# Last attention pair refilled with gates and modulation blocks, and attention results stored split

## The chip, the cores and the metric

The kernel runs on one core of one Trainium2 chip. The metric is device time in microseconds of one execution of the whole kernel: a median over repeated executions, and beside it one execution that was taken by the hardware profiler and from which every row of the trace comes. Engines are called as in the profile: PE (TensorE matmul), DVE (VectorE), ACT (ScalarE), POOL (GpSimd), SP (SyncE, which here issues most transfers).

## The reference

One layer of a hybrid network is computed for 64 sample tokens and 1024 prompt tokens (1088 columns in all), width 1024, in fp32. Cut to what the change touches:

```
mod  = silu(c) @ w_ada + b_ada                        # 48 blocks of 128 channels: shifts, scales, gates
u    = rmsnorm(x) * (1 + sc1) + sh1
proj = u @ w_in                                       # q, k, v, mLSTM inputs, and ga, gb (1024 each)
y_a  = stick_breaking(q, k, v)                        # 8 heads of 64, strictly causal
         z = q k^T / 8 ; a = sigmoid(z) * prod over later keys of sigmoid(-z) ; y = a v
y_b  = mlstm(...)                                     # 4 heads of 128
merged = sigmoid(ga) * (y_a @ w_a) + sigmoid(gb) * (y_b @ w_b)
x    = x + g1 * (merged @ w_out)
x    = x + g2 * ffn(rmsnorm(x) * (1 + sc2) + sh2)     # then a last rmsnorm
```

## The kernel before

Every matmul operand is split into a high part (rounded to the matmul format fp32r) and a low part (the rest), and one product is three matmuls: high by high, high by low, low by high (`mm3`). Activations lie transposed, channels on partitions, and the 1088 columns are walked in three token chunks of 320, 384 and 384.

The stages in order: modulation blocks 0 to 15, the norm and the operands `uh`, `ul`; the mLSTM branch, whose results go to `yb_d` in device memory already split; the attention stage, which is where the change lies; branch A (`y_a @ w_a`, merged with the rest); the output projection; the FFN; the last norm.

The attention stage works in four pairs of heads. `attention(p)` loads the operands of the two heads, then for a head takes eight query tiles of 128 in four steps m of two. For a query tile t: two matmuls for each 512 keys give `z` (PE), DVE adds the mask on the diagonal block, ACT takes two sigmoids, DVE runs a running product along the keys (the scan) and a multiply. Then PE transposes blocks of the result (`ps_a`), ACT rounds them (`ah`), DVE subtracts (`al`), PE multiplies with v (`po`), ACT and DVE put the two halves together in `ya`. Work grows with t: tile t has t+1 key blocks, 36 in a head and 72 in a pair. Between the two heads `sample()` does the 64 sample tokens against the cache. A pair ends with one store of `ya` to `ya_d`.

Beside it run *fillers*, work that needs nothing of attention: a gate unit (`gate_unit`: one 128-channel block of ga or gb over three chunks, 24 matmuls a chunk; ACT takes the sigmoid out of PSUM into a tile with the tag "gt", SP stores it) and modulation blocks (`ada_unit`: one 512 KB weight load, a few small matmuls). Gates and modulation blocks share two PSUM banks with the tag "d". There are 16 gates; two are done earlier, and the pairs 0, 1 and 2 get 5, 5 and 4 of them with 6, 8 and 8 modulation blocks. The last pair has the last eight modulation blocks and `branch_b` (24 products of 12 matmuls, which also use the "d" banks; each takes a gate tile back from memory, multiplies it on POOL and stores the product; two "gt" tiles each, of four). In three of its steps `branch_b` calls `load_y`, which brings back `ya` of the pairs 0 to 2 and splits it on POOL.

What sets the order: the program is written as generators. `run(consumer, dense, 27, 0)` with a last argument of 0 writes the whole consumer (the pair) first and then all its fillers. A scheduler then lays out a queue for each engine while the program is built: it takes what it holds to be ready by its own model, and what was written first goes first; tiles of one tag are given out in the order written. On the chip each engine runs its queue strictly in order. So the rows of a queue are a fact of the program, and only their times are open.

Of the kernel before, what the change touches and what calls it, by code (L numbers as in the profile page):

```python
# [35 lines left out]
def trunk(ctx, tc, a, o, dbg=None, stop=None):  # L36
# [105 lines left out]

    ya_d = dram.tile([3, P, T], F32, name="ya_d")
    yb_d = dram.tile([4, 2, P, T], F32, name="yb_d")
# [67 lines left out]

    def ada_blocks(blocks, tag, nb, load):

        n = len(blocks)
        i0, step = blocks[0], blocks[-1] - blocks[0]
        ps = bank(tag, f"ps_ada{i0}", nb)
        for b, i in enumerate(blocks):
            raw = load(i)
            nc.sync.dma_start(raw, cols(w_ada, i * P))  # L220
            for kb in range(KB):
                g = 32 * (kb % 4)
                nc.tensor.matmul(ps[g : g + 32, b * P : (b + 1) * P], cT[:, kb, :], raw[:, kb, :],
                                 start=kb < 4, stop=kb >= 4, tile_position=(0, g))
        sb = small([P, n * P], f"ada_sb{i0}", "adas")
        nc.vector.tensor_copy(sb, ps[:, 0 : n * P])
# [121 lines left out]

    def unit(name, fills, evac, alloc=None):
        wh, wl = w_unit(fills, name)  # L350
        if alloc:
            alloc()
        for c, (s, e) in enumerate(CHUNKS):
            ps = bank("d", f"ps_{name}_{c}", cur["d"])
            for kb in range(KB):
                mm3(ps[:, : e - s], wh[:, kb, :], wl[:, kb, :], uh[kb][:, s:e], ul[kb][:, s:e], kb == 0, kb == KB - 1)
            evac(ps, s, e)
            yield

    def w_cols(c0):  # L360
        return lambda raw: [(raw, cols(w_in, c0))]
# [82 lines left out]
    def attention(p):  # L444
# [73 lines left out]
        for i in range(2):  # L518
            qs, kh, kl, vs = hd[i]
            for m in range(4):  # L520
                avs = []
# [45 lines left out]
        if p < 3:  # L567
            nc.sync.dma_start(ya_d[p], ya)

# [255 lines left out]
    def gate_unit(b, c0, dst, name):  # L825
        def fin(ps, s, e):
            t = small([P, 384], f"gt_{name}{b}_{s}", "gt", bufs=cur["gt"])
            nc.scalar.activation(t[:, : e - s], ps[:, : e - s], AF.Sigmoid)  # L828
            nc.sync.dma_start(dst[b][:, s:e], t[:, : e - s])
        return unit(f"{name}{b}", w_cols(c0 + b * P), fin)  # L830

# [140 lines left out]
    def load_y(b):  # L972
        y_tiles(b)
        if b >= 4:
            for i, t in enumerate((yh[b], yl[b])):
                nc.sync.dma_start(t.bitcast(F32), yb_d[b - 4, i])
            return
        raw = up.tile([P, T], F32, tag="u", name=f"yr{b}")
        nc.sync.dma_start(raw, ya_d[b])
        for s, e in CHUNKS:  # L980
            hi_pool(yh[b][:, s:e], raw[:, s:e])
            lo_pool(yl[b][:, s:e], raw[:, s:e], yh[b][:, s:e])

# [6 lines left out]
    def branch_b():  # L990

        for m in range(KB):
            if m % 2 == 0:
                wh, wl = wb0 if m == 0 else wide_unit(w_b, 0, 4, m // 2, f"wb{m}")
            if 2 <= m < 5:
                load_y(m - 2)
            for c, (s, e) in enumerate(CHUNKS):
                n = e - s
# [11 lines left out]
    gi, ai = 2, 2  # L1010
    for p, (ng, na) in enumerate(((5, 6), (5, 8), (4, 8))):
        gs, ads = gates[gi : gi + ng], ada_left[ai : ai + na]
        gi, ai = gi + ng, ai + na
        fill = []
        for i in range(na):
            fill += gs[i : i + 1] + ads[i * na // ng : (i + 1) * na // ng]
        run(attention(p), chain(fill), 27, 0)
    wb0 = wide_unit(w_b, 0, 4, 0, "wb0")
    for b in range(4, 8):
        load_y(b)  # L1020
    run(attention(3), chain(ada_left[24:32] + [branch_b()]), 27, 0)
    ph.close()

# [34 lines left out]
    for m4 in range(0, KB, 4):  # L1058
        if m4:
            early_x = {m: wo_x(m) for m in range(2)}  # L1060
        was = [wide_unit(w_a, 0, 4, m // 2, f"wa{m}", hi_act, lo_dve) for m in (m4, m4 + 2)]
        for c, m in [(c, m4 + i) for c in range(3) for i in range(4)]:
# [682 lines left out]
```

## Time and profile before

| what | us |
|---|---|
| median of three executions (1789.58 to 1793.16) | 1790.57 |
| the profiled execution, its own time | 1792.89 |
| its span, first to last instruction | 1790.7 |
| mean granted TensorE clock | 0.984 |
| PE busy in the span | 1725.0 (96%) |
| DVE / ACT / POOL busy | 1039.5 / 745.5 / 539.0 |
| first matmul of attention pairs 0, 1, 2, 3 | 506.7, 591.2, 691.9, 784.4 |
| branch B, first to last matmul | 824.6 to 897.4 |
| branch A, first to last matmul | 897.6 to 949.1 |
| first matmul of the output projection | 949.2 |

Matmuls are pipelined and their ends are modelled, so PE counts as busy in the trace where it is merely in flight. The step from one matmul's start to the next is the better measure of what it costs, and that is what is used below. Times inside the trace are microseconds from the span's start.

### The profile page before, as it was taken

The page shows a single profiled execution, that of the slowest core. Times are in us where ns is not written, and L with a number is a line of the kernel's source. Part 1 is how long each engine was busy: PE and PEld are TensorE (multiplying, and loading weights), DVE is VectorE, ACT ScalarE, POOL GpSimd, SP SyncE. Part 2 cuts the span into 40 slices and gives each one's busy share as a digit, 9 for nine tenths or more (in the row PEclk, how much of TensorE's full clock was granted, in tenths as well). Part 3 has the DMA queues.
Part 4 walks back from the last instruction along what each step waited for, and adds up shares of the span by engine and source line. Part 5 has one row for each costly group of instructions (what it writes and reads, how often), then busy time and mean ns, then how long its engine had stood idle before and what let it go on. Part 6 is the DMA issues. An engine that isn't in the chain of part 4 may idle for free. (4 is left out here: it accounts for less than half of the span.)

```text
span 1790.7 us, 32772 instructions
## 1 busy us (share of the span) xinstructions
PE 1725.0 (96%) x12670; PEld 1661.6 (93%) x12670; DVE 1039.5 (58%) x2029; ACT 745.5 (42%) x1511; POOL 539.0 (30%) x491
## 2 busy tenths in 40 slices
PE   6999999999999999988899999999999999999998
PEld 4899999999989989877899999999999999999998
DVE  5533324152356858586554389666655677667964
ACT  6333333324234535353423457432333355453444
POOL 1434544445532232314656240044322100001000
PEclk9999999999999999998999999999999999999999
DMA  9436666664485565695576345744433588899942
GB/s 276 113 103 205 149 197 143 192 146 138 149 199 137 135 165 130 140 270 182 169 232 195 98 138 166 203 145 154 147 99 98 157 235 235 283 340 338 302 149 101
DMA packets 359534, 320.25 MB, mean 179 GB/s; under 512 B 16727, under 2 KB 327507, under 8 KB 359379
## 3 DMA queue, kind: packets, MB, share of 16 engines
q1 hardware_dynamic: 345074, 270.77, 50.2%
q0 software_dynamic: 14304, 47.39, 10.6%
q8 instruction: 100, 1.64, 0.4%
q14 instruction: 56, 0.45, 0.1%
HBM read 241.01 MB, written 98.09 MB: 189 GB/s over the span
## 5 line engine op out<-in xcount | busy, mean ns | idle before, releaser
L1627 PE MATMUL ps_d<-o,wh_d 128*128 128x272 f32 x1232 | 230.9, 287 | 0.8 <-DVE g L1388 0.8
L1627 PEld LDWEIGHTS ps_d<-o,wh_d 128*128 128x128 f32 x1232 | 192.7, 188 | 1.0 <-DVE g L1388 1.0
L1627 PE MATMUL ps_d<-o,wl_d 128*128 128x272 f32 x616 | 176.4, 288 | 0.0
L1627 PEld LDWEIGHTS ps_d<-o,wl_d 128*128 128x128 f32 x616 | 115.5, 188 | 0.0
L47 ACT CAST w<-wr 128x512 fp32r<-128x512 f32 x140 | 84.8, 618 | 66.3 <-PE ps_gc L1400 17.5
L56 DVE TENSOR_TENSOR w<-wr,w 128x512 fp32r<-128x512 f32 x140 | 95.5, 696 | 22.4 <-ACT w L47 20.1
L399 DVE TENSOR_TENSOR_SCAN re<-re 128x128 f32<-128x128 f32 (+3 forms) x64 | 100.8, 1577 | 13.1 <-ACT re L395 12.7
L1611 POOL DMA_DIRECT2D dsum_d<-wr_d x12 | 6.5, 538 | 240.5 <-DVE wr_d L1609 235.7
L395 ACT ACTIVATE re<-z 128x512 f32<-128x512 f32 (+2 forms) x96 | 47.4, 494 | 72.8 <-DVE z L391 59.2
L1400 PE MATMUL ps_ga<-b1h,w 128*128 128x272 f32 x352 | 74.7, 289 | 3.0 <-ACT g L1385 1.8
L1400 PE MATMUL ps_gc<-b5h,w 128*128 128x272 f32 x352 | 75.1, 292 | 1.1 <-DVE g L1388 1.1
L1400 PE MATMUL ps_gd<-b4h,w 128*128 128x272 f32 x352 | 74.1, 290 | 1.2 <-DVE hst L1382 1.2
L1400 PE MATMUL ps_gb<-b6h,w 128*128 128x272 f32 x352 | 74.2, 289 | 0.1
L1400 PE MATMUL ps_gd<-b7h,w 128*128 128x272 f32 x352 | 74.2, 290 | 0.0
L1400 PE MATMUL ps_gc<-b3h,w 128*128 128x272 f32 x352 | 73.7, 289 | 0.0
L1400 PE MATMUL ps_ga<-b2h,w 128*128 128x272 f32 x352 | 73.6, 288 | 0.0
L47 ACT CAST o<-hr 128x544 fp32r<-128x544 f32 x77 | 48.8, 645 | 52.0 <-DMA hr<-h_d 28.8
L47 ACT CAST wh_d<-wr_d 128x1024 fp32r<-128x1024 f32 (+1 forms) x42 | 41.1, 979 | 69.4 <-PE ps_d L1627 32.2
L76 PE MATMUL ps_ga<-uh,wh_ga 128*128 128x384 f32 (+1 forms) x192 | 65.4, 340 | 4.4 <-ACT gt_ga L828 3.6
L56 DVE TENSOR_TENSOR o<-hr,o 128x544 fp32r<-128x544 f32 x77 | 53.9, 723 | 20.7 <-ACT o L47 20.3
L76 PE MATMUL ps_gb<-uh,wh_gb 128*128 128x384 f32 (+1 forms) x192 | 65.0, 339 | 0.0
L78 PE MATMUL ps_ga<-uh,wl_ga 128*128 128x384 f32 (+1 forms) x192 | 64.3, 335 | 0.0
(557 smaller groups left out, 5865.2 us busy)
## 6 DMA issues: line engine op xcount, KB each, us to landing
wada<-in_w_ada SPq DMA_DIRECT2D x48, 512.0 KB
wr<-wsum_d SPq DMA_DIRECT2D x80, 256.0 KB
wr_d<-in_w_ff_down SPq DMA_DIRECT2D x34, 512.0 KB
h_d<-hst SPq DMA_DIRECT2D x44, 272.0 KB
wr<-in_w_ff_gate SPq DMA_DIRECT2D x40, 256.0 KB
hr<-h_d SPq DMA_DIRECT2D x33, 272.0 KB
wsum_d<-in_w_ff_up POOLq DMA_DIRECT2D x6, 1282.0 KB, 7.7
wsum_d<-in_w_ff_gate POOLq DMA_DIRECT2D x6, 1282.0 KB, 7.9
```

Source lines behind the costliest of these rows:

```text
L47: nc.scalar.copy(out, in_)
L56: nc.vector.tensor_sub(out, in_, h.bitcast(F32))
L76: nc.tensor.matmul(ps, wh, xh, start=first, stop=False)
L78: nc.tensor.matmul(ps, wl, xh, start=False, stop=last)
L395: nc.scalar.activation(rest[:, c0 : c0 + w], ps, AF.Sigmoid, scale=-scale)
L399: nc.vector.tensor_tensor_scan(r, r, r, 1.0, ALU.mult, ALU.bypass)
L1400: nc.tensor.matmul(ps, w[:, a, j, :], b[j // 2][:, j % 2, :], start=p in (1, 6, 5, 7) and j == 0 and k == 0, stop=j == 3 and k == 2, skip_ ...
L1611: nc.gpsimd.dma_start(dsum_d[p][mp, ks[0] // 4][:, : P * n], flat)
L1627: nc.tensor.matmul(ps, a[:, j, mi, :], b[:, h], start=p not in (2, 4) and k == ks[0] and i == 0, stop=k == ks[-1] and i == 2, skip_group_c ...
```

## The change

Five things change, all in the attention stage and at the start of branch A:

1. **Attention results are stored split.** At the end of pairs 0 to 2, `ya` is split on POOL chunk by chunk (three high and three low tiles), and six stores go to `ya_d`, now twice as large. `load_y` becomes two plain loads. The six tiles have the tag "gt" with four buffers: the same buffers as those of the gates' sigmoids.
2. **Fillers are dealt out anew.** Pairs 0, 1 and 2 get 4, 4 and 4 gates (6, 8, 8 modulation blocks as before). The last pair is written in two parts: 14 steps (head 0 and the sample tokens); then four modulation blocks, a gate, four more blocks, the weights of branch B, the last gate; then head 1 and branch B. The last gate's chunks 1 and 2 run together on the two banks (`last=True`).
3. **The last pair's operands come by token chunks:** the mLSTM results (`yh[4..7]`, `yl[4..7]`) are loaded in 24 pieces instead of eight whole tiles, and branch B goes chunk by chunk over four output blocks instead of block by block.
4. **The last head's steps run backwards,** m = 3, 2, 1, 0.
5. **Branch A's first weights** take their low part on POOL instead of DVE.

The core of the diff:

```diff
-    ya_d = dram.tile([3, P, T], F32, name="ya_d")
+    ya_d = dram.tile([3, 2, P, T], F32, name="ya_d")
...
-            for m in range(4):
+            for m in (range(4) if (p, i) != (3, 1) else range(3, -1, -1)):
...
         if p < 3:
-            nc.sync.dma_start(ya_d[p], ya)
+            for s, e in CHUNKS:
+                h_, l_ = (small([P, 384], f"ys{x}{p}_{s}", "gt", F32R, bufs=4)[:, : e - s] for x in "hl")
+                hi_pool(h_, ya[:, s:e])
+                lo_pool(l_, ya[:, s:e], h_)
+                nc.sync.dma_start(ya_d[p, 0, :, s:e], h_.bitcast(F32))
+                nc.sync.dma_start(ya_d[p, 1, :, s:e], l_.bitcast(F32))
...
     def load_y(b):
         y_tiles(b)
-        if b >= 4:
-            for i, t in enumerate((yh[b], yl[b])):
-                nc.sync.dma_start(t.bitcast(F32), yb_d[b - 4, i])
-            return
-        raw = up.tile([P, T], F32, tag="u", name=f"yr{b}")
-        nc.sync.dma_start(raw, ya_d[b])
-        for s, e in CHUNKS:
-            hi_pool(yh[b][:, s:e], raw[:, s:e])
-            lo_pool(yl[b][:, s:e], raw[:, s:e], yh[b][:, s:e])
+        for i, t in enumerate((yh[b], yl[b])):
+            nc.sync.dma_start(t.bitcast(F32), ya_d[b, i])
...
-        for m in range(KB):
-            if m % 2 == 0:
-                wh, wl = wb0 if m == 0 else wide_unit(w_b, 0, 4, m // 2, f"wb{m}")
-            if 2 <= m < 5:
-                load_y(m - 2)
-            for c, (s, e) in enumerate(CHUNKS):
+        left = 3
+        for m4 in range(0, KB, 4):
+            wbs = [wb0 if m == 0 else wide_unit(w_b, 0, 4, m // 2, f"wb{m}") for m in (m4, m4 + 2)]
+            for i, (c, m) in enumerate((c, m4 + i) for c in range(3) for i in range(4)):
+                (s, e), (wh, wl) = CHUNKS[c], wbs[m % 4 // 2]
+                if left and i >= 3 and i % 3 == 0:
+                    load_y(3 - left)
+                    left -= 1
...
-    for p, (ng, na) in enumerate(((5, 6), (5, 8), (4, 8))):
+    for p, (ng, na) in enumerate(((4, 6), (4, 8), (4, 8))):
+        run(attention(p), chain(gates_ada(ng, na)), 27, 0)
+
+    last_pair = attention(3)
+    for _ in range(14):
+        next(last_pair)
+    fill = ada_left[ai : ai + 4] + gates[gi : gi + 1] + ada_left[ai + 4 :]
+    for _ in chain(fill):
+        pass
     wb0 = wide_unit(w_b, 0, 4, 0, "wb0")
+    for _ in gates[gi + 1]:
+        pass
     for b in range(4, 8):
-        load_y(b)
-    run(attention(3), chain(ada_left[24:32] + [branch_b()]), 27, 0)
+        y_tiles(b)
+    for s, e in CHUNKS:
+        for b in range(4, 8):
+            for i, t in enumerate((yh[b], yl[b])):
+                nc.sync.dma_start(t[:, s:e].bitcast(F32), yb_d[b - 4, i, :, s:e])
+    run(last_pair, branch_b(), 27, 0)
...
-        was = [wide_unit(w_a, 0, 4, m // 2, f"wa{m}", hi_act, lo_dve) for m in (m4, m4 + 2)]
+        was = [wide_unit(w_a, 0, 4, m // 2, f"wa{m}", hi_act, lo_dve if m4 else lo_pool) for m in (m4, m4 + 2)]
```

In the queues the change moves far more than the diff shows. Three places follow. In the names, `z0_0_4_0` is pair 0, head 0, query tile 4, keys from 0; `ps_a0_0_1_0` is pair 0, head 0, step m = 1, key blocks from 0; `po` and `ya` are numbered in the same way; `ga2` is the third gate, `ada19` a modulation block; the last number only counts tiles.

**PE, the first pair.** Before, at its fifth query tile:

```order
L78 MATMUL ps_ga3_2_5634<-uh6_137,wl_ga3_5575 128x384
L76 MATMUL ps_ga3_2_5634<-uh7_139,wh_ga3_5574 128x384
L77 MATMUL ps_ga3_2_5634<-ul7_140,wh_ga3_5574 128x384
L529 MATMUL z0_0_4_0_4979<-kh0_0_4861,qs0_0_4860 128x512
L530 MATMUL z0_0_4_0_4979<-kl0_0_4862,qs0_0_4860 128x512
L78 MATMUL ps_ga3_2_5634<-uh7_139,wl_ga3_5575 128x384
L223 MATMUL ps_ada19_5662<-wada19_5663,cT_85 32x128
L543 MATMUL ps_a0_0_1_0_4951<-ident_66,be_0_0_2_4932 128x128
L529 MATMUL z0_0_4_512_4982<-kh0_0_4861,qs0_0_4860 128x128
L530 MATMUL z0_0_4_512_4982<-kl0_0_4862,qs0_0_4860 128x128
```

Now, from the last filler that stands ahead of the pair:

```order
L78 MATMUL ps_ga2_1_5517<-uh7_139,wl_ga2_5486 128x384
L541 MATMUL z0_0_0_0_4890<-kh0_0_4861,qs0_0_4860 128x128
L541 MATMUL z0_0_1_0_4901<-kh0_0_4861,qs0_0_4860 128x256
L542 MATMUL z0_0_0_0_4890<-kl0_0_4862,qs0_0_4860 128x128
L542 MATMUL z0_0_1_0_4901<-kl0_0_4862,qs0_0_4860 128x256
L541 MATMUL z0_0_2_0_4928<-kh0_0_4861,qs0_0_4860 128x384
L542 MATMUL z0_0_2_0_4928<-kl0_0_4862,qs0_0_4860 128x384
L541 MATMUL z0_0_3_0_4939<-kh0_0_4861,qs0_0_4860 128x512
L542 MATMUL z0_0_3_0_4939<-kl0_0_4862,qs0_0_4860 128x512
L555 MATMUL ps_a0_0_0_0_4913<-ident_66,be_0_0_0_4894 128x128
L555 MATMUL ps_a0_0_0_0_4913<-ident_66,be_0_0_1_4905 128x128 x2
```

Gate chunks and modulation blocks stood between the attention matmuls of the first pair. Now no filler follows the second chunk of the gate `ga2` until the pair is through.

**ACT, and PE behind it: when the sigmoid of that gate is taken.** ACT before, around the start of the first pair:

```order
L828 ACTIVATE gt_ga1_704_4835<-ps_ga1_2_4810 128x384
L828 ACTIVATE gt_ga2_0_5497<-ps_ga2_0_5472 128x320
L828 ACTIVATE gt_ga2_320_5525<-ps_ga2_1_5500 128x384
L828 ACTIVATE gt_ga2_704_5553<-ps_ga2_2_5528 128x384
L828 ACTIVATE gt_ga3_0_5603<-ps_ga3_0_5578 128x320
L395 ACTIVATE re_0_0_0_4895<-z0_0_0_0_4890 128x128
L396 ACTIVATE be_0_0_0_4894<-z0_0_0_0_4890 128x128
L395 ACTIVATE re_0_0_1_4906<-z0_0_1_0_4901 128x256
L396 ACTIVATE be_0_0_1_4905<-z0_0_1_0_4901 128x256
```

ACT now, the rows that hold the same sigmoid; `yo0_1_3` is the last copy of pair 0:

```order
L568 COPY yo0_1_3_5462<-po0_1_3_5410 64x256
L406 ACTIVATE re_1_0_4_6066<-z1_0_4_512_6061 128x128
L407 ACTIVATE be_1_0_4_6065<-z1_0_4_512_6061 128x128
L47 CAST ah_1_0_1_0_6035<-ps_a1_0_1_0_6030 128x512
L47 CAST ah_1_0_1_2_6047<-ps_a1_0_1_2_6043 128x384
L568 COPY yo1_0_0_6004<-po1_0_0_5991 64x256
L406 ACTIVATE re_1_0_5_6082<-z1_0_5_0_6074 128x512
L407 ACTIVATE be_1_0_5_6081<-z1_0_5_0_6074 128x512
L845 ACTIVATE gt_ga2_0_5514<-ps_ga2_0_5489 128x320
L845 ACTIVATE gt_ga2_320_5542<-ps_ga2_1_5517 128x384
```

PE now, where the third chunk of the same gate stands:

```order
L562 MATMUL po1_0_1_6029<-al_1_0_1_2_6048,vs1_0_5942 128x256
L562 MATMUL po1_0_1_6029<-ah_1_0_1_2_6047,vs1_0_5942 128x128
L562 MATMUL po1_0_1_6029<-al_1_0_1_2_6048,vs1_0_5942 128x128
L76 MATMUL ps_ga2_2_5545<-uh0_125,wh_ga2_5485 128x384
L77 MATMUL ps_ga2_2_5545<-ul0_126,wh_ga2_5485 128x384
L78 MATMUL ps_ga2_2_5545<-uh0_125,wl_ga2_5486 128x384
```

The sigmoids of the gate's first two chunks moved from the start of pair 0 to behind its last copy. Its third chunk moved on PE from ahead of the pair to behind step m = 1 of head 0 of pair 1. The fillers of the pairs 1 and 2 moved in the same way: they stand behind the next pair's first query tiles.

**PE, the end of the last pair.** Before:

```order
L77 MATMUL ps_b7_0_9510<-yl7_8317,wh_wb6_9449 128x320
L550 MATMUL po3_1_3_8878<-al_3_1_3_4_8911,vs3_1_8334 128x256
L550 MATMUL po3_1_3_8878<-ah_3_1_3_4_8910,vs3_1_8334 128x256
L550 MATMUL po3_1_3_8878<-al_3_1_3_4_8911,vs3_1_8334 128x256
L550 MATMUL po3_1_3_8878<-ah_3_1_3_6_8922,vs3_1_8334 128x256
L78 MATMUL ps_b7_0_9510<-yh7_8316,wl_wb6_9450 128x320
L550 MATMUL po3_1_3_8878<-al_3_1_3_6_8923,vs3_1_8334 128x256
L550 MATMUL po3_1_3_8878<-ah_3_1_3_6_8922,vs3_1_8334 128x128
L550 MATMUL po3_1_3_8878<-al_3_1_3_6_8923,vs3_1_8334 128x128
L76 MATMUL ps_b7_1_9529<-yh4_8304,wh_wb6_9449 128x384
```

Now:

```order
L76 MATMUL ps_gb7_2_8783<-uh7_139,wh_gb7_8750 128x384
L77 MATMUL ps_gb7_2_8783<-ul7_140,wh_gb7_8750 128x384
L78 MATMUL ps_gb7_2_8783<-uh7_139,wl_gb7_8751 128x384
L562 MATMUL po3_1_0_9112<-al_3_1_0_0_9118,vs3_1_8183 128x256
L562 MATMUL po3_1_0_9112<-ah_3_1_0_0_9117,vs3_1_8183 128x128
L562 MATMUL po3_1_0_9112<-al_3_1_0_0_9118,vs3_1_8183 128x128
L76 MATMUL ps_b0_0_9136<-yh4_8838,wh_wb0_8744 128x320
L77 MATMUL ps_b0_0_9136<-yl4_8839,wh_wb0_8744 128x320
L78 MATMUL ps_b0_0_9136<-yh4_8838,wl_wb0_8745 128x320
L76 MATMUL ps_b0_0_9136<-yh5_8840,wh_wb0_8744 128x320
```

Before, branch B stood between the last pair's matmuls. Now the last two gates and the last eight modulation blocks stand there, and branch B follows whole behind the last attention matmul.

More of the change, by code (lines that the diff above doesn't have):

```diff
@@ L211, in trunk, with ada_blocks @@
     p0 = open_phase("start")
-    def ada_blocks(blocks, tag, nb, load):
+    def ada_blocks(blocks, tag, nb, load, new_bank=None, new_small=None):
         n = len(blocks)
         i0, step = blocks[0], blocks[-1] - blocks[0]
-        ps = bank(tag, f"ps_ada{i0}", nb)
+        ps = (new_bank or (lambda name: bank(tag, name, nb)))(f"ps_ada{i0}")
         for b, i in enumerate(blocks):
@@ L224, in ada_blocks @@
                                  start=kb < 4, stop=kb >= 4, tile_position=(0, g))
-        sb = small([P, n * P], f"ada_sb{i0}", "adas")
+        sb = (new_small or (lambda name: small([P, n * P], name, "adas")))(f"ada_sb{i0}")
         nc.vector.tensor_copy(sb, ps[:, 0 : n * P])
@@ L347, in evac_v, with unit @@
         nc.scalar.copy(pairs[p].vf[:, s:e], ps[:, : e - s])
-    def unit(name, fills, evac, alloc=None):
+    def unit(name, fills, evac, alloc=None, last=False):
         wh, wl = w_unit(fills, name)
@@ L353, in unit @@
         for c, (s, e) in enumerate(CHUNKS):
+            if last and c:
+                break
             ps = bank("d", f"ps_{name}_{c}", cur["d"])
@@ L357, in unit @@
             evac(ps, s, e)
+            yield
+        if last:
+            pss = [bank("d", f"ps_{name}_{c}", cur["d"]) for c in (1, 2)]
+            for kb in range(KB):
+                for ps, (s, e) in zip(pss, CHUNKS[1:]):
+                    mm3(ps[:, : e - s], wh[:, kb, :], wl[:, kb, :], uh[kb][:, s:e], ul[kb][:, s:e], kb == 0, kb == KB - 1)
+            for ps, (s, e) in zip(pss, CHUNKS[1:]):
+                evac(ps, s, e)
             yield
@@ L829, in fin @@
             nc.sync.dma_start(dst[b][:, s:e], t[:, : e - s])
-        return unit(f"{name}{b}", w_cols(c0 + b * P), fin)
+        return unit(f"{name}{b}", w_cols(c0 + b * P), fin, None, name == "gb" and b == KB - 1)
     def in_unit(name, c0, i, evac, alloc):
@@ L1010, in trunk, with gates_ada @@
     gi, ai = 2, 2
-    for p, (ng, na) in enumerate(((5, 6), (5, 8), (4, 8))):
+    def gates_ada(ng, na):
+        nonlocal gi, ai
         gs, ads = gates[gi : gi + ng], ada_left[ai : ai + na]
@@ L1016, in trunk @@
             fill += gs[i : i + 1] + ads[i * na // ng : (i + 1) * na // ng]
-        run(attention(p), chain(fill), 27, 0)
+        return fill
+    for p, (ng, na) in enumerate(((4, 6), (4, 8), (4, 8))):
[6 more added lines that the diff above has]
+        pass
     wb0 = wide_unit(w_b, 0, 4, 0, "wb0")
+    for _ in gates[gi + 1]:
+        pass
     for b in range(4, 8):
-        load_y(b)
-    run(attention(3), chain(ada_left[24:32] + [branch_b()]), 27, 0)
+        y_tiles(b)
[4 more added lines that the diff above has]
+    run(last_pair, branch_b(), 27, 0)
     ph.close()
```

## The prediction

> **What bounds the kernel now.** I read the profile's page first, then the busy times by stage, then the waits of PE, then the groups of DVE, and last the queues of both kernels, which the sections ahead show in part.
>
> ```profile
> span 1790.7 us, 32772 instructions
> PE 1725.0 (96%) x12670; PEld 1661.6 (93%) x12670; DVE 1039.5 (58%) x2029; ACT 745.5 (42%) x1511; POOL 539.0 (30%) x491
> ```
>
> PE bounds the kernel as a whole. The change touches only the stretch from 491.3 us (where the PE queues of both kernels part) to 949.2 us (first matmul of the output projection): 457.9 us. Busy time by stage there:
>
> ```profile
> core 0: us, PE busy (x) PEld busy (x) DVE busy (x) ACT busy (x) POOL busy (x), PEclk, DMA share, GB/s
> 491.30:506.70 15.40, 11.73 (x67) 10.96 (x66) 0.78 (x4) 1.31 (x3) 6.47 (x13) 0.78 1.24 272
> 506.70:784.40 277.70, 269.15 (x1914) 246.91 (x1912) 197.03 (x378) 129.29 (x300) 84.65 (x85) 0.99 0.60 149
> 784.40:824.60 40.20, 31.88 (x286) 23.80 (x282) 31.96 (x80) 18.51 (x42) 3.60 (x3) 0.83 0.84 268
> 784.40:897.60 113.20, 97.99 (x698) 86.97 (x695) 75.82 (x148) 52.42 (x121) 55.46 (x48) 0.94 0.65 208
> 790.00:800.00 10.00, 7.41 (x46) 5.87 (x46) 9.91 (x25) 7.20 (x17) 0.56 (x1) 1.00 1.05 394
> 897.60:949.20 51.60, 49.43 (x289) 48.84 (x288) 31.00 (x56) 14.21 (x33) 27.04 (x25) 0.97 0.78 234
> ```
>
> The first three pairs (506.7 to 784.4) keep PE busy. The last pair does not: in 784.4 to 824.6, one head with nothing but modulation blocks beside it, PE is busy 31.88 of 40.2 and the granted clock is 0.83. At its densest (790 to 800) DVE is busy 9.91 of 10 and PE 7.41: a head without dense fillers is bound by DVE, and in its tail by the chain PE, ACT, DVE, PE. That is the rate to keep in mind.
>
> What a matmul costs PE, from start to start:
>
> ```profile
> 519.71 0.41 PE L223 MATMUL ps_ada<-wada,cT 128*32 128x128 f32 x6
> 520.05 0.50 PE L529 MATMUL z<-kh,qs 128*128 128x512 f32 x1
> ...
> 521.07 0.31 PE L76 MATMUL ps_ga<-uh,wh_ga 128*128 128x320 f32 x1
> 521.22 0.31 PE L77 MATMUL ps_ga<-ul,wh_ga 128*128 128x320 f32 x1
> ...
> 533.21 0.33 PE L76 MATMUL ps_ga<-uh,wh_ga 128*128 128x384 f32 x1
> 533.38 0.33 PE L77 MATMUL ps_ga<-ul,wh_ga 128*128 128x384 f32 x1
> ...
> 535.60 0.28 PE L550 MATMUL po<-ah,vs 128*128 128x256 f32 x1
> 535.72 0.28 PE L550 MATMUL po<-al,vs 128*128 128x256 f32 x1
> ```
>
> So 0.15 us for 320 columns, 0.173 for 384, 0.12 for 256, others in proportion (not under 0.1), and 0.34 for six of the sixteen matmuls of a modulation block, 0.9 for all. A gate is 24 x (0.147 + 2 x 0.173) = 11.9 us, branch B and branch A 47.4 each (288 matmuls), attention 29 a pair. Over the pairs 0 to 2 the queue before holds 253 us of such work in 277.7 us: 0.91. The last pair holds 87 in 113.2: 0.77.
>
> **The change: what decides.** The six tiles of the split results share the four "gt" buffers with the gates' sigmoids and are written first, so the queues shown ahead put the sigmoids of a pair's first gate behind the pair's last copy. That gate's two chunks fill both "d" banks; every later gate chunk and modulation block needs one. So PE gets attention alone. I went through the new PE queue and summed each stretch with the steps above. Three stretches are bare: from the first `z` of pair 0 to step m = 1 of head 0 of pair 1 (93 key blocks, 34.5 us of PE work); from head 1 of pair 1 to the same place in pair 2 (56 blocks, 19.4 us); from the third last query tile of pair 2 to the same place in pair 3 (42 blocks, 16.2 us). That is 191 of 288 key blocks, 5.3 heads, with 70 us of PE work. What DVE needs for them:
>
> ```profile
> L399 DVE TENSOR_TENSOR_SCAN re<-re 128x128 f32<-128x128 f32 (+7 forms) x48 | 78.2, 1631 | 11.1 <-ACT re L395 10.8
> L400 DVE TENSOR_TENSOR be<-be,re 128x128 f32<-128x128 f32 (+7 forms) x48 | 39.1, 815 | 3.1 <-ACT re L395 0.5
> L56 DVE TENSOR_TENSOR al<-ps_a,ah 128x512 fp32r<-128x512 f32 (+1 forms) x57 | 35.1, 630 | 16.1 <-ACT ah L47 15.7
> L391 DVE TENSOR_TENSOR z<-z,amask 128x128 f32<-128x128 f32 x48 | 13.9, 294 | 14.7 <-PE z L530 14.4
> L557 DVE TENSOR_TENSOR ya<-po,yo 64x256 f32<-64x256 f32 x22 | 9.2, 418 | 15.1 <-ACT yo L556 13.0 <-DMA ya_d<-ya 1.6
> ```
>
> These are six heads (48 query tiles): 78.2 + 39.1 + 35.1 + 13.9 + 9.2 = 175.5, so 29 us a head, 30 with the small ones left out. The sample tokens have the work of a query tile of five key blocks, 30 x 5 / 36 = 4, and the split of the cache: an estimate of 6. The bare stretches hold 5.3 x 30 + 1.5 x 6 = 168 us of DVE work. Some of it is slowed by POOL in this trace:
>
> ```profile
> 770.73 2.39 POOL L59 TENSOR_TENSOR wl_wb<-wr_wb,wh_wb 128x1024 fp32r<-128x1024 f32 x1
> 770.99 4.01 DVE L399 TENSOR_TENSOR_SCAN re<-re 128x896 f32<-128x896 f32 x1
> ...
> 801.27 2.02 DVE L399 TENSOR_TENSOR_SCAN re<-re 128x896 f32<-128x896 f32 x1
> ```
>
> The same scan takes 4.01 beside POOL's weight split and 2.02 without. With the short durations throughout, a head is 27.5 and the stretches 154. That is the lower end (156 at 0.99 busy). The upper end is the rate of the starved head, DVE busy 31.96 of 40.2, 0.80: 168 / 0.80 = 210. I take 0.94, nearer to the dense row, since no modulation block waiting for its weights stands in the way: **178 us**, where PE has 70 us to do. The 108 us between them are the price of the change.
>
> The start: before, PE stood 3.57 us for the gate's sigmoid and went on at half speed, and the first operands of attention arrived at 503.2:
>
> ```profile
> 491.25 0.34 PE L78 MATMUL ps_ga<-uh,wl_ga 128*128 128x384 f32 x1
> 495.15 0.69 PE L76 MATMUL ps_ga<-uh,wh_ga 128*128 128x384 f32 x1 [3.57 <-ACT gt_ga L828]
> 495.64 0.53 PE L77 MATMUL ps_ga<-ul,wh_ga 128*128 128x384 f32 x1
> 495.96 0.53 PE L78 MATMUL ps_ga<-uh,wl_ga 128*128 128x384 f32 x1
> ...
> 503.23 0.37 DVE L479 CAST zq<-qs 128x64 fp32r<-128x64 f32 x1
> ```
>
> Now the next row on PE after 491.3 is the first `z`, which needs those operands: **12.5 us** of nothing, to 503.8.
>
> The rest of PE's work up to branch B is gates 158.2 (13 and a chunk), modulation blocks 26.8 (30), attention 46.3: 231.3 us. The pairs 0 to 2 ran at 0.91. The stretch of the last pair has chains between few fillers, as 0.77 shows, so I take 0.89 over all: **260 us** (0.95 gives 244, 0.85 gives 272).
>
> Branch B now runs bare, with two "gt" tiles for each product and four buffers. A product is 1.98 us on PE. What the buffers allow shows in the last products of before:
>
> ```profile
> 889.02 0.32 SPq L1003 DMA_DIRECT2D lgb<-gb_d  x1
> ...
> 889.51 0.87 POOL L1006 TENSOR_TENSOR tb<-tb,lgb 128x320 f32<-128x320 f32 x1 [2.08 <-DMA lgb<-gb_d]
> ...
> 901.71 1.01 POOL L1006 TENSOR_TENSOR tb<-tb,lgb 128x384 f32<-128x384 f32 x1 [0.50 <-DMA lgb<-gb_d]
> ```
>
> From product 18 to product 23, five in 12.2 us, 2.44 each, is 58.6 for 24; PE alone is 47.4. I take **54 us** (48 to 60). In it are branch A's low parts, now on POOL between the products, at about the 2.4 us that the row of `wl_wb` has. Branch A keeps its **51.6** (50 to 53).
>
> Edits at nothing. The split itself: 18 POOL instructions are removed from `load_y` and the same 18 stand at the ends of pairs. Twice the bytes, 3.3 MB more in some 500 us at 149 to 208 GB/s, lie beside compute; without that cover they would be some 20 us. SP issues 15 more stores and 16 more operand pieces, 0.32 us each as in the row above, 10 us in the whole stage; behind them wait weight loads that run three tiles ahead. The backward last head shortens a tail that branch B covers.
>
> Sum: 12.5 + 178 + 260 + 54 + 51.6 = 556 against 457.9: 98 us more. The profiled execution took 1792.89 with its span of 1790.7, 2.3 over the median; I put the 98 on the median: 1790.6 + 98 = 1889.
>
> A page of the Trainium skill speaks of the bare stretches too. The row is the clock of 0.83 from 784.4 to 824.6, and the steps of 0.32 instead of 0.17 after the wait at 491.25. "TensorE: Matmul & The Clock Gate" (Part 1) has the clock at half after an idle window of about 3.4 us, and its Part 4 says that transposes do not count as PE activity in the same way; a third of a head's matmuls are transposes. The trace agrees with the first, and with the second as far as the starved head shows. By that rule the clock would be at half through most of the bare stretches, which is the second rival.
>
> **The rivals.**
> - *DVE runs through and the fillers run clean.* For it: 9.91 of 10. Against it: the tails, where DVE waits for ACT (`al` 15.7 us, `ya` 13.0). 12.5 + 156 + 244 + 48 + 50 = 510: 52 more, 1843.
> - *The bare stretches run at the starved rate,* with PE's 70 us at half clock becoming 140 in chain with DVE, and the fillers start slow each time. For it: 40.2 us for one head at 0.83. Against it: modulation blocks held that head up. 14 + 210 + 272 + 60 + 53 = 609: 151 more, 1942.
> - *Faster: the banks come free after all.* If the gates' sigmoids could run within the pair, the fillers would interleave as before, and the last pair, with two gates in place of waits, would run at 0.91: 87 / 0.91 = 96 instead of 113.2, and branch A's first waits are 2 us: 1772. It decides from the point where ACT takes `ga2`'s sigmoid ahead of the pair's last copy. The ACT rows ahead say the opposite, and a queue is in order.
> - *It all cancels,* within 0.2% (3.6 us, about what a measurement of this kernel can tell from no change): the bare stretches would have to hold no more PE idle than before had. Their DVE work alone, 154 to 168 against 70, forbids it.
>
> **How the numbers follow.** My forecast 0.60; starved rate 0.20; DVE through 0.15; faster 0.03; no change 0.02. Slower is 0.60 + 0.20 + 0.15 = 0.95. The forecast is 1889. The range runs between the two slower rivals, which hold the unknown rates: 1843 to 1940.
>
> **What would show it.** In the profile after: PE lines of idle before `z`, `ps_a` and `po` in the first pair, with DVE busy above 0.9 and PE below 0.5 in the 90 us after the first `z`; no `gt_ga` sigmoid in that time; gate chunks in runs of 24 behind pair 1's first query tiles; branch B some 54 us long without attention in it; everything behind the output projection unchanged. I am wrong if gates run within the first pair, if a bare head takes under 27 us, or if the loss sits elsewhere.

## The result and the profile after

The changed kernel takes 1878.95 us (1874.48 to 1882.64) against 1790.07 us (1788.53 to 1793.16) in the same session: a ratio of 1.0493, 95% interval 1.0466 to 1.0520. Slower, as forecast; the 1889 of the forecast was 10 us too much. The line numbers below are those of the changed kernel, 12 higher than before in `attention` (`z` is now L541 and L542) and 17 higher at the gates' sigmoids (L845).

The page of the changed kernel: span, busy time of each engine, and the 40 slices of PE and of its clock.

```profile
span 1877.7 us, 32842 instructions
PE 1759.9 (94%) x12670; PEld 1681.2 (90%) x12670; DVE 1028.2 (55%) x2027; ACT 748.2 (40%) x1511; POOL 537.3 (29%) x493
PE   6999999999778989799789999999999999999998
PEclk9999999999768979899899999999999999999999
```

The matmuls are as many as before. The loss stands in slices 11 to 21 of 46.9 us, where PE's digit falls to 7 and the clock's to 6: the attention pairs, and in slices 20 and 21 the start of branch B. Busy time by stage there, cut at the first `z` and at the first and last of each run of gate matmuls:

```profile
core 0: us, PE busy (x) PEld busy (x) DVE busy (x) ACT busy (x) POOL busy (x), PEclk, DMA share, GB/s
490.80:499.70 8.90, 0.36 (x3) 0.07 (x2) 0.19 (x1) 0.00 (x0) 3.33 (x7) 0.70 1.29 227
499.70:586.10 86.40, 63.12 (x268) 48.31 (x269) 69.65 (x133) 46.59 (x111) 22.90 (x32) 0.68 0.49 104
586.10:648.50 62.40, 62.25 (x467) 59.11 (x466) 23.14 (x48) 17.65 (x39) 20.20 (x17) 1.00 0.62 153
648.50:693.20 44.70, 33.13 (x152) 25.93 (x151) 38.35 (x77) 25.08 (x60) 13.93 (x18) 0.73 0.37 87
693.20:763.40 70.20, 69.72 (x528) 64.20 (x527) 34.30 (x74) 22.41 (x51) 19.08 (x18) 1.00 0.61 156
763.40:799.60 36.20, 25.26 (x130) 21.04 (x130) 31.63 (x62) 22.07 (x52) 13.88 (x18) 0.81 0.46 110
799.60:916.90 117.30, 108.92 (x848) 97.36 (x846) 61.97 (x133) 37.37 (x84) 23.74 (x15) 0.97 0.46 132
916.90:987.30 70.40, 54.58 (x291) 51.60 (x291) 4.17 (x5) 14.60 (x31) 32.38 (x29) 0.90 0.75 247
987.30:1037.50 50.20, 48.08 (x289) 47.27 (x288) 28.94 (x52) 13.32 (x30) 23.37 (x22) 1.00 0.80 238
```

The second, fourth and sixth rows are the three bare stretches (attention alone on PE), 167.3 us together; the rows between them, with the gates back, keep PE busy throughout. The last two rows are branch B and branch A. The output projection starts at 1037.5 instead of 949.2, 88.3 us later; behind it nothing changed (1877.7 - 1037.5 = 840.2 against 1790.7 - 949.2 = 841.5).

The first gate sigmoid after the first `z`, on ACT's timeline:

```profile
584.74 0.83 ACT L845 ACTIVATE gt_ga<-ps_ga 128x320 f32<-128x320 f32 x2
```

It comes 85 us after the first `z`; PE's next gate matmul follows 1.4 us later. The four largest of PE's waits between 490.8 and 799.6 (us in total, times, longest):

```profile
PE po L562 <- DVE al L56: 11.9, 12, 2.0
PE z L541 <- ACT be L407: 11.7, 16, 2.0
PE z L541 <- DMA kh<-qk_d: 8.5, 1, 8.5
PE ps_ys L523 <- DVE ys L521: 6.1, 3, 2.5
```

The 8.5 us are the start, where the first `z` waits for its operand. The others are attention's own waits, none longer than 2.5 us; no gate stands here, since the gates come behind the bare work in PE's queue.

### The profile page after: what moved, and what is told of

Same layout as the page of the kernel before. It is cut to its first block, busy times and chain, and to the rows that moved or that the text cites. A ratio compares the mean times of both kernels' runs of the same rounds, so it can differ in the third digit from the quotient of the medians.

```text
span 1877.7 us, 32842 instructions
## 1 busy us (share of the span) xinstructions
PE 1759.9 (94%) x12670; PEld 1681.2 (90%) x12670; DVE 1028.2 (55%) x2027; ACT 748.2 (40%) x1511; POOL 537.3 (29%) x493
## 5 line engine op out<-in xcount | busy, mean ns | idle before, releaser
L410 DVE TENSOR_TENSOR_SCAN re<-re 128x128 f32<-128x128 f32 (+3 forms) x64 | 91.7, 1437 | 5.9 <-ACT re L406 5.6
L562 PE MATMUL po<-al,vs 128*128 128x256 f32 (+1 forms) x160 | 51.5, 352 | 18.6 <-DVE al L56 16.1
L541 PE MATMUL z<-kh,qs 128*128 128x512 f32 (+2 forms) x96 | 44.5, 467 | 21.9 <-ACT be L407 11.7
```

Source lines behind the costliest of these rows:

```text
L410: nc.vector.tensor_tensor_scan(r, r, r, 1.0, ALU.mult, ALU.bypass)
L541: nc.tensor.matmul(z[:, :w], q, kh[:, NS + k0 : NS + k0 + w], start=True, stop=False)
L562: nc.tensor.matmul(po[:, 256 - n : 256], vs[:, j, :], x[:, w : w + n], start=j == 0 and x is ah, stop=j == last and x is al)
```

## The experiments

### Whose buffers cost the time

Theory: the split costs nothing of itself; the four buffers that it shares with the gates' sigmoids cost all of it. Rival: the 18 POOL instructions, the 15 more stores and the doubled bytes, or the order of gates, blocks and products. Four kernels take it apart.

*The changed kernel with buffers of its own for the split* (two of 320 columns, the split in four pieces):

```diff
-            for s, e in CHUNKS:
-                h_, l_ = (small([P, 384], f"ys{x}{p}_{s}", "gt", F32R, bufs=4)[:, : e - s] for x in "hl")
+            for s, e in ((0, 320), (320, 576), (576, 832), (832, T)):
+                h_, l_ = (small([P, 320], f"ys{x}{p}_{s}", "ysp", F32R, bufs=2)[:, : e - s] for x in "hl")
```

> The changed kernel, but the split attention results have a tag of their own (two buffers of 320 columns, four pieces a pair) instead of the gates' four buffers. Theory (the shared buffers hold the gates' sigmoids behind the pair's end, and that alone makes the loss): gates stand between the attention matmuls again, PE waits in the first three pairs fall back to about 25 us, 1765 to 1785 us. Rival (the loss comes from the new deal of fillers, the operands by chunks or the backward head): still 1865 to 1885 us.

Measured: 1795.3 us, ratio to before 1.0022 (1.0004 to 1.0040), 10 us over the expected range. No bare stretch is left, and ACT takes 12 of the gates' sigmoids in the first 80 us behind the first `z`, where the changed kernel has none:

```profile
505.70:609.70 104.00, 99.50 (x684) 90.75 (x684) 74.29 (x142) 45.38 (x107) 41.04 (x40) 0.97 0.70 172
609.70:790.00 180.30, 169.46 (x1303) 152.97 (x1303) 135.24 (x278) 86.67 (x201) 64.83 (x68) 0.98 0.62 161
```

*The kernel before with the split alone, through the gates' buffers* (the same store and the direct load, nothing else of the change):

```diff
-            nc.sync.dma_start(ya_d[p], ya)
+            for s, e in CHUNKS:
+                h_, l_ = (small([P, 384], f"ys{x}{p}_{s}", "gt", F32R, bufs=4)[:, : e - s] for x in "hl")
+                hi_pool(h_, ya[:, s:e])
...
```

> The kernel before with one part of the change: results stored split through the gates' buffers, and loaded split. Theory: the same three bare stretches (their 100 us over PE's own work), no gates left for the last pair: 1870 to 1895 us. Rival (the other parts make the loss): 1785 to 1795 us.

Measured: 1868.35 us, ratio 1.0426 (1.0403 to 1.0449), 2 us under the expected range.

*The same with buffers of its own* (`"ysp"`, four pieces, as above):

> The kernel before with the results stored split through a tag of their own (two buffers of 320 columns). Theory: the split itself costs nothing and takes POOL's 18 instructions out of branch B's time: 1780 to 1791 us. Rival (POOL's splits or the doubled stores at the end of a pair cost): 1800 us or more.

Measured: 1790.18 us, ratio 0.9995 (0.9978 to 1.0012). 

*The changed kernel without the split* (stored whole; split on POOL when it is loaded, as before):

```diff
-            for s, e in CHUNKS:
-                h_, l_ = (small([P, 384], f"ys{x}{p}_{s}", "gt", F32R, bufs=4)[:, : e - s] for x in "hl")
...
+            nc.sync.dma_start(ya_d[p], ya)
```

> The changed kernel without its first part: results stored whole as before and split on POOL when loaded; the fillers, the chunks, the backward head and the weights stay changed. Theory: 1765 to 1785 us. Rival (those other parts make the loss): 1865 to 1885 us.

Measured: 1783.11 us, ratio 0.9960 (0.9946 to 0.9974).

What follows: the shared buffers are the cause. Against the same split with buffers of its own they cost 78 us in the kernel before (1868.35 - 1790.18) and 84 us in the changed one (1878.95 - 1795.29). The split through buffers of its own costs nothing in the kernel before that the interval of 0.2% would show. The rest of the change, without the split, makes the kernel 0.4% faster, which is the fastest version found and beats both kernels. So the theory holds for the kernel before and not wholly for the changed one: there the split with its own buffers still costs some 12 us (1795.29 - 1783.11); where, the last experiments ask.

### Each pair pays for itself

```diff
-            for s, e in CHUNKS:
-                h_, l_ = (small([P, 384], f"ys{x}{p}_{s}", "gt", F32R, bufs=4)[:, : e - s] for x in "hl")
+            for s, e in CHUNKS if p == 0 else ((0, 320), (320, 576), (576, 832), (832, T)):
+                h_, l_ = ((small([P, 384], f"ys{x}{p}_{s}", "gt", F32R, bufs=4) if p == 0 else
+                           small([P, 320], f"ys{x}{p}_{s}", "ysp", F32R, bufs=2))[:, : e - s] for x in "hl")
```

> The changed kernel, but only the split of pair 0 is written through the gates' buffers; pairs 1 and 2 split through two small buffers of their own. Theory (each pair pays for itself: a pair whose split shares the gates' buffers runs its attention alone up to its last copy): the first bare stretch stays (86 us, 52 of them more than its 34.5 us of PE work), the second and third (25 and 20 more than their PE work) go. Of the 84 us between the kernel with own buffers for all (1795.3) and the changed kernel (1879), 52 / 97 stay: 45, so 1840 (1833 to 1848). Rival (the gates catch up: what is late in pair 0 is hidden by the richer filling of the later pairs): 1795 to 1815. Rival (the price is that gates end up in the last pair and branch B runs without attention, whichever pair pushed them there): 1860 to 1880.

Measured: 1839.41 us, ratio 1.0260 (1.0240 to 1.0281). Its windows from the first `z` to branch B:

```profile
502.50:587.50 85.00, 61.02 (x269) 46.73 (x269) 69.49 (x133) 46.63 (x111) 23.18 (x32) 0.71 0.50 105
587.50:746.00 158.50, 156.46 (x1175) 144.65 (x1175) 90.12 (x176) 57.64 (x130) 51.40 (x46) 1.00 0.60 155
746.00:874.00 128.00, 116.17 (x858) 101.63 (x857) 85.60 (x176) 54.53 (x125) 44.38 (x41) 0.97 0.58 157
```

One stretch of 85 us is left, the others are gone, and the time lies 44 us over the kernel with own buffers for all pairs, where 45 were expected. Later pairs do not make up for an earlier one.

### What sets the length of a bare stretch

The forecast took DVE's work at 0.94 busy; a rival took PE at half clock as part of the chain. In the windows both look possible: DVE is busy 0.81, 0.86 and 0.87 of the three, and PE, at a granted clock of 0.68 to 0.81, 0.70 to 0.74. Two kernels add work to the one and take work from the other.

*PE: `z` of pair 0 three times into the same bank.*

```diff
+                        for _ in range(3 if p == 0 else 1):
...
```

> The changed kernel with each pair of z matmuls of pair 0's full query tiles issued three times into the same bank (the last gives the same z). This adds 128 x 36 key blocks x 2 heads x 4 matmul columns = 36900 columns, 17 us of PE work at the step of 0.15 us for 320 columns and 35 us at half of it, all in the first bare stretch (86.4 us, PE busy 63 at a granted clock of 0.68, DVE busy 70). Theory (the stretch is set by DVE and the waits between the engines, and PE's half clock costs little): the stretch grows by 0 to 8 us, the granted clock rises, time 1879 to 1887. Rival (PE at half clock is the bound): it grows by 17 to 35 us, time 1896 to 1914. Third (PE's idle windows are the price, and keeping it busy pays): the stretch gets shorter, under 1877.

*DVE: without the multiplication of `beta` by the running product* (attention's result then lacks that factor).

```diff
         nc.vector.tensor_tensor_scan(r, r, r, 1.0, ALU.mult, ALU.bypass)
+        if mask is amask:
+            return rest[:, 1 : n + 1]
         nc.vector.tensor_mul(beta, beta, rest[:, 1 : n + 1])
```

> The changed kernel without DVE's multiplication of beta by the running product in the full query tiles of all pairs (the running product itself is used as the weights, so attention's result leaves that factor out). The multiplication took 815 ns for 48 tiles in three pairs before, 6.5 us a head; 5.3 bare heads hold 35 us of it. Theory (DVE sets the bare stretches): they fall from 167 us to 137 (130 to 145), the rest of the kernel stays, time 1849 (1841 to 1858). Rival (PE at half clock in chain with ACT sets them): they fall by under 10 us, time 1869 to 1880.

Measured: 1893.58 us (ratio 1.0562, 1.0541 to 1.0584) with `z` three times, 1857.19 us (1.0360, 1.0338 to 1.0382) without the multiplication. The first total lies between the ranges of the theory and of the rival, the second just inside the theory's range, so the stretches have to be read. With `z` three times:

```profile
502.30:591.10 88.80, 72.22 (x358) 59.27 (x358) 68.55 (x129) 45.47 (x107) 23.64 (x32) 0.82 0.47 98
653.90:701.30 47.40, 32.51 (x158) 24.62 (x156) 41.36 (x78) 25.96 (x63) 16.76 (x20) 0.82 0.41 102
767.80:815.00 47.20, 34.67 (x157) 27.46 (x155) 40.45 (x77) 25.96 (x65) 15.71 (x19) 0.75 0.49 110
```

The first stretch, the only one with the added work, holds 358 matmuls instead of 268 and lasts 88.8 us instead of 86.4; its clock rose from 0.68 to 0.82. So 90 more matmuls cost 2.4 us. That is a balance, though: at the higher clock the transposes of the stretch took 329 ns on average instead of 366, so part of the added work was paid back by a faster chain, and the run does not show that PE is off the chain. The time was lost in the third stretch, which grew by 11 us with 157 matmuls instead of 130 and 77 DVE instructions instead of 62. No `z` was added there. The scheduler that lays out the queues had put the cut elsewhere and left more attention bare. I had not expected that an edit in pair 0 moves the cut in pair 2.

Without the multiplication:

```profile
502.50:578.50 76.00, 57.02 (x267) 44.30 (x267) 55.32 (x110) 45.01 (x108) 21.28 (x32) 0.75 0.56 118
641.10:678.30 37.20, 27.61 (x155) 21.84 (x153) 32.76 (x65) 24.30 (x60) 15.82 (x19) 0.91 0.50 116
748.40:775.80 27.40, 21.07 (x129) 16.05 (x127) 24.64 (x51) 20.99 (x51) 12.30 (x18) 1.00 0.62 146
```

The three stretches last 140.6 us instead of 167.3: 26.7 less. DVE's busy time in them fell from 139.6 to 112.7: 26.9 less. In the sum that is one for one, and what remains beside DVE's work is 27.7 us in the changed kernel and 27.9 us here. Stretch by stretch it is not: 10.4 us shorter for 14.3 of DVE, 7.5 for 5.6, 8.8 for 7.0. The clock rose here too (to 0.75, 0.91 and 1.00), and with `z` three times the remainder is 33.0 us (183.4 less 150.4). So DVE's work sets most of a bare stretch, and the exact sum is in part chance; how much of the remainder is PE's slower clock stays open. The kernel gave back 21.8 of the 26.7 us (24.0 when each is taken against the kernel before in its own session). The multiplication that I had put at 35 us for these stretches has records of 32 us there, part of it beside other records of DVE.

### Why branch B took 70 us

The forecast was 54, by the pace that four buffers allow. Product by product, POOL's multiplications at the start of branch B in the changed kernel show something else:

```profile
931.13 1.67 POOL L1018 TENSOR_TENSOR tb<-tb,lgb 128x320 f32<-128x320 f32 x2 [10.89 <-DMA lgb<-gb_d]
941.84 0.86 POOL L1018 TENSOR_TENSOR tb<-tb,lgb 128x320 f32<-128x320 f32 x1 [9.04 <-issue]
944.18 0.86 POOL L1018 TENSOR_TENSOR tb<-tb,lgb 128x320 f32<-128x320 f32 x1 [1.48 <-DMA lgb<-gb_d]
```

Branch B starts at 916.9. Its first two products wait for their gate tiles until 931.1, and the third is multiplied at 941.8. What PE waited for in branch B, what SP waited for before it asked for the operand pieces (L1050), and the copy of the fourth product:

```profile
PE ps_b L76 <- ACT tb L1017: 14.6, 6, 6.5
PE ps_b L76 <- DMA yh<-yb_d: 1.0, 1, 1.0
SPq L1050 <- PE ps_gb L78: 4.9, 4, 3.6
942.24 0.42 ACT L1017 COPY tb<-ps_b 128x320 f32<-128x320 f32 x1 [8.98 <-DMA pb_d<-tb]
```

PE stood 14.6 us for banks and about 1 us for operands. A bank comes free with ACT's copy, the copy needs one of the four "gt" buffers, and these are held by products whose gate tile has not arrived or whose store (`pb_d`) has not landed. Busy time of branch B in two pieces:

```profile
916.90:945.00 28.10, 14.85 (x69) 13.03 (x69) 4.17 (x5) 4.10 (x11) 6.61 (x6) 0.81 0.96 334
945.00:987.30 42.30, 39.73 (x224) 38.57 (x223) 0.00 (x0) 10.50 (x21) 25.77 (x24) 0.96 0.60 189
```

The transfers of the first piece (packets, then issues: count, KB each):

```profile
DMA packets 5716, 9.40 MB, mean 334 GB/s; under 512 B 593, under 2 KB 4946, under 8 KB 5714
...
yh<-ya_d SPq DMA_DIRECT2D x3, 544.0 KB
yl<-ya_d SPq DMA_DIRECT2D x3, 544.0 KB
yh<-yb_d SPq DMA_DIRECT2D x8, 192.0 KB
```

In the first 28.1 us the 16 DMA engines are busy 0.96 and PE 14.9 us. Most of branch B's operands and all of attention's split results pass here. They could not come earlier: `uh` and `ul` hold all sixteen "u" buffers until the last gate, for which SP waits in the third row of waits, and the change moved that gate to just ahead of branch B. After that the pace is 42.3 us for 224 matmuls, 12 to a product: 2.27 us each, so 54 us for 24, the forecast. In the kernel before with the split alone these loads are issued from 874 to 906 and branch B starts at 919.4. It takes close to that pace's time, and PE stands 6.1 us for banks instead of 14.6:

```profile
919.40:977.60 58.20, 51.68 (x288) 48.72 (x289) 3.81 (x8) 13.02 (x27) 29.95 (x27) 0.97 0.62 197
```

So the 16 us by which the forecast was too low are a start-up, in which gate tiles and stores wait beside the operands' transfers. Is it the order on SP, so that a better one would save it, or the bytes? Three kernels change the order in the changed kernel. In what follows, numbered products (product 3, product 12) are counted from 0.

*The pieces of the second and third chunk behind the first and second product, attention's results asked for in the second half:*

```diff
+                if m4 == 0 and i < 2:
+                    yb_pieces(i + 1)
...
-                if left and i >= 3 and i % 3 == 0:
+                if left and m4 and i >= 3 and i % 3 == 0:
```

> The changed kernel with branch B's loads in another order: ahead of it only the 8 operand pieces of the first chunk, the 8 of the second behind the first product, the 8 of the third behind the second product, and attention's results from the second half of branch B on. Theory (the 70 us of branch B instead of the 48 that PE has are a start-up: the gates' loads for products 0 to 3 stand behind 24 pieces and six whole-width loads on SP): branch B falls to 58 us (54 to 63), time 1867 (1862 to 1872). Rival (four buffers for two tiles a product set the pace, as forecast): branch B stays at 68 to 71, time 1876 to 1881.

*Attention's results held back behind products 12, 15 and 18, by a write into each tile that waits for the product:*

```diff
+            hi_pool(t[:, 0:8], src[:, 0:8])
...
+                if left and m4 and i % 3 == 0:
+                    load_y(3 - left, t)
```

> The changed kernel with attention's split results loaded behind products 12, 15 and 18 of branch B, held back by a small write into each tile that waits for the product's own multiplication; the pieces stay in one run ahead of branch B. The order before this one moved only what the queue's planner left: the six whole-width loads still stood ahead of the gate load of product 4. Theory (these six loads, 3.3 MB, hold up the gate loads behind them by some 10 us): branch B falls from 70 us to 60 (57 to 64), time 1869 (1866 to 1873). Rival (branch B is bound by the bytes: 4.4 MB of pieces, 3.3 MB of results and 2 x 24 gate tiles have to pass in it in any order): 67 to 71 us, 1876 to 1880.

*Both* (results held back, pieces behind the products):

> Both orders at once in the changed kernel: attention's results held back behind products 12, 15 and 18, and the pieces of the second and third chunk behind the first and second product. Theory (two start-up costs that add: the six loads some 10 us, the 24 pieces ahead of the first gate load some 5): branch B 55 us (52 to 59), time 1864 (1860 to 1868). Rival one (the pieces cost nothing, as the order alone showed no gain): branch B and the time as with the results late alone, 1867 to 1872. Rival two (bytes): 67 to 71, 1876 to 1880.

Measured: 1881.85 us (ratio 1.0502, 1.0483 to 1.0521) with the pieces moved, 1887.20 us (1.0534, 1.0515 to 1.0552) with the results held back, 1887.12 us (1.0536, 1.0514 to 1.0559) with both. Branch B took 72.4, 73.6 and 76.1 us. The theory of the order falls: none was faster, and all three lie above even the rivals' ranges. In the first of them the scheduler had still put the six whole-width loads ahead of the gate load of product 4, which is why the second holds them back by data. There the start is better (product 3 is multiplied 19 us behind the start of branch B, 27 before), and the time goes again later, on POOL:

```profile
966.31 0.86 POOL L1016 TENSOR_TENSOR tb<-tb,lgb 128x320 f32<-128x320 f32 x1 [2.56 <-DMA lgb<-gb_d]
971.32 1.77 POOL L1016 TENSOR_TENSOR tb<-tb,lgb 128x320 f32<-128x320 f32 x2 [4.15 <-DMA lgb<-gb_d]
981.75 2.07 POOL L1016 TENSOR_TENSOR tb<-tb,lgb 128x384 f32<-128x384 f32 x2 [5.40 <-DMA lgb<-gb_d]
```

Each two loads of 0.56 MB make the gate tile behind them late. At the 334 GB/s of the row above they take 3.3 us, and with four buffers for two tiles a product the gate tiles can run only about one product, 2 us, ahead. The changed kernel and these three move 17.2 to 17.7 MB in branch B, the kernel before with the split alone 11.4 MB. So it looks as if the bytes have to pass somewhere in branch B, and wherever they pass it stands; that is argued from these rows, and whether more gate buffers would bridge it was not tried.

### The same order where attention covers it

*Own buffers for the split, with the new order of the first of the three kernels:*

> The kernel with buffers of its own for the split (1795.3), with the operand pieces of the second and third chunk behind the first and second product of branch B, and attention's results loaded from its second half on. Theory (what this kernel loses against the one without the split, 1783.1, lies in branch B, which took 76.4 us from first to last matmul against 70.8, because the whole-width loads of the split results stand ahead of the gates' loads): 1789 (1786 to 1791.5). Rival (it lies in the pairs, where the split's extra stores and POOL work stand, or in nothing that this order touches): 1793 to 1798.

*The fastest version, without the split, with the pieces behind the products:*

> The changed kernel without the split (1783.1), with the operand pieces of the second and third chunk behind the first and second product of branch B. It is tried as the fastest. PE waited there for branch B's banks 2.1 us in three waits. Theory: these waits go and no other takes their place, 1781 (1779 to 1783). Rival (the pieces are now late for product 4, or nothing hangs on these waits): 1783 to 1787.

Measured: 1789.54 us, ratio 0.9987 (0.9974 to 0.9999), and 1789.99 us, ratio 0.9998 (0.9981 to 1.0016). The first is 0.35% better than without the order (1.0022), as expected: 5.8 of the 12 us that the split still cost came back, 4.3 of them in branch B (76.6 us, now 72.3). The rest stays open. The second is worse than without it (0.9960) and above the ranges of both theory and rival: branch B took 75.6 us instead of 71.0, and PE's waits there for branch B's banks came to 4.1 us instead of 2.1. The same edit gained in one kernel and lost in another, so I have no rule for this order.

## Why the prediction was right, step by step

| Step | forecast, us | measured, us |
|---|---|---|
| start wait | 12.5 | 8.9 |
| three bare stretches | 178 | 167.3 |
| the rest of PE's work | 260 | 249.9 |
| branch B | 54 | 70.4 |
| branch A | 51.6 | 50.2 |
| sum | 556 | 546.7 |

Four terms came out 26 us below the forecast together and branch B 16 us above it, so the total is 10 us off in part because errors offset each other.

- *The cause* was right: shared buffers, sigmoids behind the pair's last copy, both banks held. The four kernels on the buffers show it, the kernel with pair 0 alone shows that it acts pair by pair, and the first sigmoid at 584.74 fits the queue. The three stretches lie where the new queue puts them.
- *The bare stretches* came within 11 us by luck: two errors met. The forecast's 168 us of DVE work are durations of groups added up. Added up in the same way, the stretches hold 75 + 44 + 36 = 155 us, the lower end of 154 and not 168. The rate of 0.94 was taken from busy times of windows, where the same stretches have 139.6 us: neighbouring records of DVE overlap a little (a subtraction of 0.69 us starts at 560.99, the next scan at 561.60), and a window counts the overlap once. In that measure the rate was 0.83, close to the starved head's 0.80 that I passed over. So the work was 28 us too high for its rate, and the rate 0.11 too high. The scan is one part. In the first stretch its group reads, with one of the two scans there that were long and what lay beside it:

```profile
L410 DVE TENSOR_TENSOR_SCAN re<-re 128x128 f32<-128x128 f32 (+7 forms) x21 | 27.6, 1317 | 2.3 <-ACT re L406 2.2
504.76 1.28 POOL L59 TENSOR_TENSOR vx<-craw_v,vx 128x512 fp32r<-128x512 f32 x1
505.01 1.86 DVE L410 TENSOR_TENSOR_SCAN re<-re 128x384 f32<-128x384 f32 x1 [0.31 <-ACT re L406]
```

  The 1317 ns can't be set against the 1631 of before as they stand, since a group's mean mixes sizes: these 21 scans cover 87 key blocks, 4.1 each, the 48 of before 4.5 each. At the sizes' own means of before the 21 would average 1529 ns, so they are 4.5 us faster. The stretch has 13.9 us less of busy time than my rates give (93 key blocks of 36 a head at 30 us, and 6: 83.5; measured 69.65). Of these some 4.5 us are the scans, some 5 the six key blocks of the 93 whose scan falls behind the stretch, and some 5.5 the overlap of records, together a little more than the 13.9.
- *The sign* "DVE above 0.9 and PE below 0.5" was wrong, at 0.81 and 0.73. A 512-column `z` steps 0.43 us in this stretch at 503.27 and 0.23 at 585.36, at the higher clock, so PE's busy share says little of how much work it has.
- *The starved-rate rival* was right in part on the clock (0.68 to 0.81 over the stretches) and wrong on the time, 210 us against 167.3. The Trainium skill, "TensorE: Matmul & The Clock Gate", Part 1, has the clock at half after an idle window of about 3.4 us. The trace agrees on the half (granted 0.50 from 540 to 550) but shows no such pause there: behind the start, the longest wait of PE in this stretch is 2.0 us. With 90 more matmuls the clock rose to 0.82 and the stretch grew by 2.4 us, so the slow clock lay mostly beside DVE's work.
- *The rest of PE's work* took 249.9 us for the 231.3 us of steps, 0.93 where I took 0.89 (by the profile's busy time, which counts work in flight, the three rows are at 1.00, 0.99 and 0.93). I carried the tails of the last pair over to it, but in the new queue those tails lie in the bare stretches, and the fillers come in long runs.
- *Branch B* is the mis-sized term, and it fell outside its own 48 to 60. The pace was right (2.27 us a product in the steady part, 54 us for all). The step that failed is "edits at nothing": the doubled bytes "lie beside compute", and the operand pieces cost no more than their issue. I had written that without cover the bytes would be some 20 us. The cover was gone, since the last gate holds the buffers until branch B begins, and pieces and results came together; the start-up cost 16 us. I had counted the pieces' issue times and not asked when their buffers come free.
- *The start*: the first `z` followed the last gate matmul by 8.9 us, and by 8.9 to 9.2 in the other kernels whose split uses the shared buffers in pair 0. I had taken the operands' arrival over from the kernel before, by the cast of `zq` at 503.23, and that row was read wrongly: it stands right behind a copy for which DVE had waited on PE, and dates DVE's queue. In the changed kernel the same cast waits for the operand itself:

```profile
503.02 0.29 DVE L226 COPY ada_sb<-ps_ada 128x128 f32<-128x128 f32 x1 [17.87 <-PE ps_ada L223]
498.28 0.19 DVE L490 CAST zq<-qs 128x64 fp32r<-128x64 f32 x1 [13.58 <-DMA qs<-qk_d]
```

  (The first row is the kernel before, the second the changed one.)
- *The rival "faster"* needed the banks to come free within the pair. With own buffers they do, and the gain in the sum of 1772 still does not come: 1795 with the split, 1783 without.

## What to carry to other kernels

When two producers share a ring of buffers, look at the order in which they are queued and not at how full the ring is: six small copies that are written at the end of a stage can hold everything behind them that uses the same ring, and here that cost 4 to 5% of the kernel, while with two small buffers of their own the kernel before lost nothing that could be measured. When a step is moved to the end of a stage, ask which buffers it keeps until then and what has to be loaded into them; its transfers then lie in the open. And test a bound by adding work to one engine and taking it from the other, reading the stretch and not the total, since a scheduler may move the cuts elsewhere; read the clock beside it, since here both edits moved it. When a sum of work is divided by a rate, take both from the same view of the profile.

## What the runs showed of the hardware that I had not expected

- Work added to PE in a stretch at a granted clock of 0.68 was almost free: 90 added matmuls cost 2.4 us and raised the clock to 0.82. Busy time taken from DVE came back one for one in the sum of three stretches (26.9 and 26.7 us), though not in each.
- PE's granted clock was 0.50 over 10 us (540 to 550) in a stretch whose longest wait, behind its start, was 2.0 us.
- With the DMA engines 0.96 busy, 9.40 MB took 28.1 us, 334 GB/s. The Trainium skill, "DMA: Bandwidth & Descriptors", Specifications, gives some 358 GB/s as one core's limit at the memory. This stretch stays below it, but the 10 us of the kernel before that the prediction quotes (790 to 800) moved 394 GB/s as the profile counts it, so the measured number is the one to go by.
- A scan on DVE is slowed by some of POOL's work and not by other work. Of the 48 scans of the pairs 0 to 2 of the kernel before, eight took over 1.3 times the shortest of their size (a 128x512 scan 3.42 us against 1.21), and each of the eight lay beside a subtraction of two tensors on POOL (L59) for more than 1 us. Beside POOL's one-tensor rounding (L53) a 128x512 scan took 1.23 us with 1.22 us of it alongside. One scan in the changed kernel goes against this, 128 columns in 0.81 us instead of 0.42 with only a rounding beside it. These subtractions are mostly the fillers' weight splits, and few of them lie in the bare stretches. POOL's busy share is much the same (0.27 in the first bare stretch, 0.30 before), so it is the kind of work that counts. This is read from the traces; no run varied it.
